# Moving the first block's weight splits to VectorE and interleaving gather and gate/up in the first expert quad

## The chip, the cores and the metric

One core of one Trainium2 chip runs the kernel. The metric is device time in microseconds (us), the median of the runs. The engines are TensorE (PE in the rows; PEld is its weight load), VectorE (DVE), ScalarE (ACT), GpSimd (POOL) and SyncE (SP), whose queue issues nearly all weight transfers.

## What is computed

Two model blocks on 256 rows of 1024 columns, in fp32. The reference, cut to what matters:

```python
def first_block(x, ...):
    h = rms_norm(x, attn_norm_w)
    x = x + hybrid_mixer(h, ...)      # w_in -> conv + state-space branch, causal attention branch, gates, w_out
    h = rms_norm(x, moe_norm_w)
    x = x + hier_moe(h, ...)          # 4 groups x 8 experts, best group, best 2 experts in it
    gate = sigmoid(rms_norm(x, ple_norm_w) @ w_ple_gate)
    ...
def hier_moe(h, ...):
    hid = silu(h @ w_gate[e]) * (h @ w_up[e])
    out += comb[:, e] * (hid @ w_down[e])
def second_block(x, ...):             # long convolution branch, attention branch, gates, w_out
```

## The kernel before

Matrices are multiplied as three products of split numbers: each weight part of 128x1024 is loaded raw (512 KB), a high half `wsh` is made by a rounding copy on ScalarE (`act`, line 152) and a low half `wsl` as raw minus high half, and a product is high x high, high x low and low x high. `Split` (line 209) does this for a chunk of 256 output columns in two parts. Where the low half is made is `pool_lo`: for the parts that the table `APL` (line 46) lists, `G.tensor_tensor` on GpSimd (line 230), otherwise `to_split` on VectorE (`tt`, line 155). `next_a` (line 471) gives `Split` the entry of `APL` for chunk n; `v_chunk` (line 458) asks for entries of its own, and there are none. `APL` lists 19 parts of the chunks 0 to 33. The very first chunk has a fixed split of its own (line 224: part 0 on VectorE, part 1 on GpSimd). The second block lists none.

The first block goes through the convolution inputs (five chunks `pxbc` with their convolution steps `cv`, `th`, `xf` on VectorE and ScalarE, and the chunks of `pv` between them), transposes `xf` (line 569), then takes for each of four head groups the chunks `pq`, `pk`, `pz`, the rotary step (lines 716 to 725, its additions on GpSimd, line 724), a state-space group and an attention group (softmax in `mx`, `pt`, `sm`; transposes line 699), then gates and output projections (`pg`, `pao`, `pso`, `pwo`).

The order on each engine is not the order of the source: a planner lays the instructions out by costs and due times, and `hp(tag)` shifts a due time by the entry of `HPD` (line 47), among them some chunks' loads and splits (`w5` by 300, `w8` and `w16` by 150). Each engine and each queue works its list in order. Matmuls marked by `pmm` (line 867) keep their order of the source on TensorE.

The experts are taken in eight quads of four. A quad (line 1051) makes a one-hot table of its 128 slots (`make_oh`), gathers the rows of x into `xe` by matmuls, two of the eight column groups of 128 at a time (`gather`, line 983, psum tile `pxe`, one half copied by ScalarE, the other by VectorE), multiplies by gate and up weights (`gate_up`, line 1013: 16 matmuls for a pair of column groups, four experts side by side), then makes the hidden layer (`thm`, `hT`), multiplies by the down weights (`pyd`) and scatters (`acc`). `combine_weights` (line 947) works out the slot weights and the overflow count `cnti`, which the weight queue loads into a register (line 1216).

A quad has 24 weight tiles of 512 KB (`eload`, line 375; the load is line 382). They go into pools whose sequence is written out (lines 365 to 373): 9 + 3 x 6 + 4 + 6 + 4 + 6 + 2 = 49 buffers, filled while the first block runs; the 50th load takes the first buffer again. The gate/up tile i of a quad holds two column groups of expert i % 4, so that the first four tiles are free when the column groups 0 and 1 have been used. The first quad's order is:

```python
    if q == 0:
        make_oh(0); gather(0); combine_weights()
    wg, wd = quad_weights(q)
    if not last:
        quad_weights(q + 1); make_oh(q + 1)
    gate_up(q, (0, 1), pg, wg)
    if q == 0: slot_weights(0)
    slot_rows(q)
    for k in range(2, KD, 2): gate_up(q, (k, k + 1), pg, wg)
```

Of the kernel before, what the change touches and what calls it, by code (L numbers as in the profile page):

```python
# [23 lines left out]
KD = 8  # L24
# [18 lines left out]
VH = (0,)  # L43
XS = 256
W0 = 50
APL = {0: (0,), 10: (0,), 16: (0,), 18: (0,), 2: (0,), 22: (1,), 23: (1,), 24: (1,), 26: (1,), 27: (0,), 28: (0,), 31: (0,), 33: (0,), 4: (1,), 5: (0, 1), 6: (0,), 8: (0, 1)}
HPD = {'L1': 300, 'an0': 20, 'ao2': 80, 'ao3': 40, 'as2': -150, 'cgt3': -20, 'chy5': -20, 'clow1': -20, 'cpg1': -300, 'cv1': 20, 'cv4': 300, 'cwo3': 10, 'cza1': 40, 'czh1': -20, 'dt': 80, 'ex2': -10, 'ga00': -80, 'ga02': -10, 'hy3': -20, 'hy4': 40, 'lc0': 80, 'lc1': 20, 'mx2': -40, 'pT1': 300, 'pe3': 300, 'r34': 150, 'rr0': -10, 'rr1': 300, 'siza1': 80, 'sm2': -20, 'so0': -80, 'sq0': -20, 'uo001': -150, 'uo011': -80, 'v2': 10, 've0': -150, 've2': -150, 've3': -10, 'w0': 20, 'w1': -10, 'w11': -150, 'w13': 40, 'w16': 150, 'w17': 300, 'w18': 80, 'w21': 40, 'w24': 150, 'w29': 80, 'w31': -10, 'w5': 300, 'w8': 150, 'w9': -150, 'xc1': -150, 'xc2': -150, 'xc3': -80, 'xo1': 300, 'xo3': -150, 'ye1': -80, 'yn0': 150, 'z1': 10}
WQ = {(1, 0, 0): 10}
PHI = ""
# [78 lines left out]
def tile_two_blocks(ctx: ExitStack, tc: tile.TileContext, a: dict, tap=None, upto="all"):  # L128
# [16 lines left out]
    def hp(tag):  # L145
        return tc.high_priority(HPD[tag]) if tag in HPD else nullcontext()
# [7 lines left out]
    def tt(out, in0, in1, op):  # L154
        return V.tensor_tensor(out=out, in0=in0, in1=in1, op=op)  # L155
# [13 lines left out]
    def psum(tag, shape, name):  # L169
        tag = PTG.get(name, tag)  # L170
        return ps.tile(shape, F32, tag=tag, bufs={"mm": 2, "sc": 4, "tr": 2}[tag], name=name)
# [223 lines left out]
    with ExitStack() as pa:  # L395
# [62 lines left out]
        def v_chunk(j):  # L458
            with hp(f"v{j}"):
                w = w0 if j == 0 else Split(hl, lambda i: a["w_vdt"][2 * j + i], KD, 260, pool_lo=APL.get(f"v{j}", ()))  # L460
            pv = [psum("mm", [P, 260], "pv") for _ in range(NT)]
# [9 lines left out]
        def next_a():  # L471
            n = next(ia)
            with hp(f"w{n}"):
                return Split(hl, lambda i: a["w_a"][2 * n + i], KD, T, pool_lo=APL.get(n, ()))

# [290 lines left out]
        for i in range(4):  # L766
            q = got["q"]
            p = proj(h, "pk")
            with hp(f"k{i}"):
                k = rope(p, "k")  # L770
# [84 lines left out]
    with ExitStack() as pm:  # L855
# [24 lines left out]
        def st(name, *sh, dt=F32):  # L880
            return mo.tile([P, NT, *sh], dt, name=name)
# [65 lines left out]
        def combine_weights():  # L947
            gd, gw, ex, w1, w2 = st("gd", 4), st("gw", 1), st("ex", 1), st("w1", 1), st("w2", 1)
            tt(gd, lg[:, :, 0:4], bc(gm, 4), OP.subtract)
            act(gd, gd, AF.Exp)  # L950
            V.tensor_reduce(out=gw, in_=gd, axis=AX.X, op=OP.add)
            V.reciprocal(gw, gw)
            oh12, tv, vv = st("oh12", 2, 8), st("tv", 2, 8), st("vv", 2, 1)
            for i in range(2):
                ts(oh12[:, :, i, :], rk, float(i), OP.is_equal)
                tt(tv[:, :, i, :], oh12[:, :, i, :], es, OP.mult)
            V.tensor_reduce(out=vv, in_=tv, axis=AX.X, op=OP.add)
            tt(ex, vv[:, :, 1, :], vv[:, :, 0, :], OP.subtract)
            act(ex, ex, AF.Exp)
            ts(w1, ex, 1.0, OP.add)  # L960
            V.reciprocal(w1, w1)
            tt(w1, w1, gw, OP.mult)
            tt(w2, w1, ex, OP.mult)
            ew = st("ew", 1, 8)
            tt(oh12[:, :, 0, :], oh12[:, :, 0, :], bc(w1, 8), OP.mult)
            tt(oh12[:, :, 1, :], oh12[:, :, 1, :], bc(w2, 8), OP.mult)
            tt(ew[:, :, 0, :], oh12[:, :, 0, :], oh12[:, :, 1, :], OP.add)
            for t in R:
                tt(comb4[:, t].rearrange("p (g e) b -> p g e b", g=4), bc(goh[:, t], 8).rearrange("p g (e b) -> p g e b", b=4),
                   ew[:, t].broadcast_to([P, 4, 8]).rearrange("p g (e b) -> p g e b", b=4), OP.mult)  # L970
                V.tensor_copy(comb[:, t, :, 4:5], rstd[:, t : t + 1].rearrange("p (q o) -> p q o", q=1).broadcast_to([P, NQ, 1]))
            V.tensor_reduce(out=cnt, in_=prk[:, 2, :], axis=AX.X, op=OP.max)
            V.tensor_copy(cnti, cnt)
# [5 lines left out]
        def fill():  # L979
            if filler is not None:  # L980
                next(filler, None)

        def gather(q):
            for k in range(0, KD, 2):
                p = psum("tr", [P, 2, P], "pxe")
                for i in range(2):
                    for t in range(NT):
                        pmm(p[:, i, :], x_t[:, t, (k + i) * P : (k + i + 1) * P], ohs[q][:, t, :], t == 0, t == 1)
                act(xe[:, k, :], p[:, 0, :], AF.Copy, scale=vc("moe_norm_w", k))
                ts(xe[:, k + 1, :], p[:, 1, :], vc("moe_norm_w", k + 1), OP.mult)  # L990

        scales, waiting, slots = {}, [], {}

        def slot_weights(q):
            pcs = psum("tr", [P, 5], "pcs")
            for t in range(NT):
                pmm(pcs, ohs[q][:, t, :], comb[:, t, q, :], t == 0, t == 1)
            cj = mo.tile([P, 4], F32, tag="cj", bufs=2, name="cj")
            cs = mo.tile([P, 1], F32, tag="cs", bufs=2, name="cs")
            hr = mo.tile([P, 1], F32, tag="hr", bufs=2, name="hr")  # L1000
            ts(hr, pcs[:, 4:5], 0.5, OP.mult)
            V.tensor_tensor_reduce(cj, pcs[:, 0:4], blk4, 2.0, 0.0, OP.mult, OP.add, cs)
            stt(cs, cs, hr, hr, OP.mult, OP.mult)
            scales[q] = hr, cs

        def slot_rows(q):
            pqt = psum("tr", [P, T], "pqt")
            for t in range(NT):
                ptranspose(pqt[:, t * P : (t + 1) * P], ohs[q][:, t, :])
            slots[q] = Q = mo.tile([P, T], F32 if q == NQ - 1 else F32R, tag="Q", name="Q")  # L1010
            V.tensor_copy(Q, pqt)

        def gate_up(q, ks, pg, wg):
            for k in ks:
                for j in range(4):
                    pmm(pg[32 * j : 32 * j + 32, :], xe[:, k, 32 * j : 32 * j + 32],
                        wg[4 * (k // 2) + j][:, k % 2, :], k == 0, k == KD - 1)
# [33 lines left out]
        def quad(q):  # L1051
            last = q == NQ - 1
            if q == 0:
                make_oh(0)
                gather(0)
                combine_weights()
            wg, wd = quad_weights(q)
            if not last:
                quad_weights(q + 1)
                make_oh(q + 1)  # L1060
            pg = psum("mm", [P, 512], "pgu")
            gate_up(q, (0, 1), pg, wg)
            while waiting:
                waiting.pop()()
            if q == 0:
                slot_weights(0)
            slot_rows(q)
            fill()
            for k in range(2, KD, 2):
                gate_up(q, (k, k + 1), pg, wg)  # L1070
                fill()
            hr, cs = scales.pop(q)
            th = mo.tile([P, T], F32, tag="Yh", name="thm")
            act(th, pg[:, 0:T], AF.Tanh, scale=hr)
            stt(th, th, 1.0, pg[:, 0:T], OP.add, OP.mult)
            stt(th, th, cs, pg[:, T:], OP.mult, OP.mult)
            if last:
                fill()
            else:
                gather(q + 1)  # L1080
            pht = psum("tr", [P, 2, P], "pht")
            for f in range(2):
                ptranspose(pht[:, f, :], th[:, f * P : (f + 1) * P])
            hT = mo.tile([P, 2, P], F32, tag="hT", name="hT")
            act(hT, pht, AF.Copy)
            if not last:
                slot_weights(q + 1)
            py = [psum("mm", [P, 512], f"pyd{c}") for c in range(2)]
            if last:
                down(q, wd, hT, py, (0, 1), (0, 1))  # L1090
                fill()
                last_scatter(q, py)
                return
            down(q, wd, hT, py, (0, 1), (0,))
            add = scatter(q, 0, py[0])
            down(q, wd, hT, py, (0, 1), (1,))
            add()
            waiting.append(scatter(q, 1, py[1]))
            if q == NQ - 2:
                waiting.pop()()  # L1100
# [86 lines left out]
        with ExitStack() as pp:  # L1187
# [29 lines left out]
            with tc.If(nover > CAP), ExitStack() as po_:  # L1217
                ov = pool(po_, "ov")
                ho = tuple(ov.tile([P, KD // 2, T], F32, tag="ho", bufs=2, name="ho") for _ in range(2))
                for k in range(KD):  # L1220
                    xo = mo.tile([P, NT, P], F32, tag="hT", name="xo")
                    ks = slice(k * P, (k + 1) * P)
# [656 lines left out]
```

## Time and profile before

| | us |
|---|---|
| median of 3 runs | 805.27 (805.26 to 809.57) |
| profiled execution | 805.95 |
| its span, first to last instruction | 804.2 |
| TensorE busy | 766.6 (95%) |
| VectorE busy | 478.6 (60%) |
| ScalarE busy | 345.0 (43%) |
| GpSimd busy | 135.1 (17%) |

All times in rows are microseconds from the span's start unless marked ns. A busy TensorE is not TensorE at its peak, since matmuls overlap and their ends are modelled. The granted clock (PEclk) is a share of full speed. A row of a timeline gives start, length, engine, line, operation, out<-in, shape and count, and in brackets the idle time of the engine before it and what ended it. A row of waits gives who waited for whom, the sum in us, the number of times and the longest.

### The profile page before, as it was taken

Reading aid. Unit: us, or ns where it says so; the run is one execution under the profiler, and the core shown is the slowest. Engines: PE = TensorE matmul, PEld = TensorE weight load, DVE = VectorE, ACT = ScalarE, POOL = GpSimd, SP = SyncE. Lnnn points to the kernel's source line nnn. Section 1 sums busy time; section 2 is a strip of 40 time slices with the busy share of each in tenths; the row PEclk is TensorE's granted clock in tenths of the full one; section 3 lists DMA queues with packets and bytes.
Section 4 is the critical chain, followed back from the end, with each engine's and each line's share of the span. In section 5 each row is a group of like instructions: output and inputs, shape, how many; then the busy total and the mean of one; then the engine's idle time right before and its main releaser. Section 6 shows DMA issues by size and latency. Waiting matters only on the chain. (4 is left out here: it accounts for less than half of the span.)

```text
span 804.2 us, 14032 instructions
## 1 busy us (share of the span) xinstructions
PE 766.6 (95%) x5515; PEld 608.9 (76%) x5515; DVE 478.6 (60%) x932; ACT 345.0 (43%) x659; POOL 135.1 (17%) x147
## 2 busy tenths in 40 slices
PE   8996989998999999999999999889999999999997
PEld 7996878786799999645534343249999878888997
DVE  6788767887752555522243433047877887866662
ACT  6573453646544443012113112047757426555541
POOL 3713631333033310000000000100112540000000
PEclk9998999999999999999999999999999999999999
DMA  7653554243279989599999999976445231632561
GB/s 258 219 185 101 184 182 156 84 153 131 80 249 329 346 327 394 227 410 413 382 384 419 417 417 409 393 317 218 124 138 195 95 131 53 191 98 82 175 189 53
DMA packets 53204, 187.19 MB, mean 233 GB/s; under 512 B 5886, under 2 KB 8190, under 8 KB 53071
## 3 DMA queue, kind: packets, MB, share of 16 engines
q1 hardware_dynamic: 52736, 184.93, 63.3%
q0 software_dynamic: 400, 1.34, 0.4%
q8 instruction: 44, 0.72, 0.3%
q14 instruction: 24, 0.20, 0.1%
HBM read 185.20 MB, written 1.05 MB: 232 GB/s over the span
## 5 line engine op out<-in xcount | busy, mean ns | idle before, releaser
L152 ACT ACTIVATE wsh<-w 128x1024 fp32r<-128x1024 f32 (+2 forms) x148 | 153.8, 1043 | 144.4 <-issue 23.4
L155 DVE TENSOR_TENSOR wsl<-w,wsh 128x1024 fp32r<-128x1024 f32 (+3 forms) x127 | 155.8, 1231 | 67.8 <-ACT wsh L152 67.5
L143 PE MATMUL pgu<-we,xe 128*32 128x512 f32 x512 | 79.9, 599 | 4.3 <-DMA we<-in_w_e 4.0
L143 PEld LDWEIGHTS pgu<-we,xe 128*32 128x32 f32 x512 | 17.6, 109 | 55.2 <-issue 30.4
L230 POOL TENSOR_TENSOR wsl<-w,wsh 128x1024 fp32r<-128x1024 f32 x19 | 45.9, 2418 | 71.6 <-ACT wsh L152 71.4
L143 PE MATMUL pg<-h,wsh 128*128 128x256 f32 x256 | 47.1, 284 | 0.0
L143 PEld LDWEIGHTS pg<-h,wsh 128*128 128x128 f32 x256 | 39.6, 189 | 0.4 <-issue 0.2
L143 PE MATMUL pwo<-wsh,mh 128*128 128x256 f32 x128 | 36.1, 283 | 0.5 <-DVE x_t L164 0.5
L143 PE MATMUL pg<-h,wsl 128*128 128x256 f32 x128 | 36.2, 283 | 0.0
L143 PEld LDWEIGHTS pxe<-oh,x_t 128*128 128x128 f32 x256 | 30.0, 191 | 8.1 <-issue 4.2
L143 PE MATMUL pwo<-wsl,mh 128*128 128x256 f32 x128 | 36.1, 283 | 0.0
L143 PE MATMUL pwo<-wsh,ml 128*128 128x256 f32 x128 | 35.9, 282 | 0.0
L143 PE MATMUL pxe<-oh,x_t 128*128 128x128 f32 x256 | 33.0, 283 | 0.9 <-DVE xe L159 0.9
L143 PE MATMUL pyd<-we,hT 128*32 128x512 f32 x256 | 31.7, 597 | 1.2 <-ACT hT L152 0.7
L164 DVE SCALAR_TENSOR_TENSOR thm<-thm,pgu 128x256 f32<-128x256 f32 x8 | 3.4, 422 | 48.1 <-ACT thm L152 48.1
L143 PE MATMUL pq<-h,wsh 128*128 128x256 f32 x128 | 29.1, 319 | 0.0
L143 PE MATMUL pxbc<-h,wsh 128*128 128x256 f32 x160 | 28.5, 281 | 0.0
L1191 POOL DMA_DIRECT2D pT__5280<-in_p x1 | 0.8, 792 | 150.7 <-DMA we<-in_w_e 150.7
L155 DVE TENSOR_TENSOR Yl<-pyd,Yh 128x512 fp32r<-128x512 f32 x14 | 9.7, 692 | 27.4 <-ACT Yh L152 27.4
L143 PE MATMUL pz<-h,wsh 128*128 128x256 f32 x128 | 25.6, 291 | 0.0
L143 PEld LDWEIGHTS pq<-h,wsh 128*128 128x128 f32 x128 | 21.3, 204 | 5.5 <-issue 4.0
L143 PEld LDWEIGHTS pwo<-wsh,mh 128*128 128x128 f32 x128 | 24.3, 190 | 0.7 <-DVE x_t L164 0.7
(473 smaller groups left out, 2125.0 us busy)
## 6 DMA issues: line engine op xcount, KB each, us to landing
we<-in_w_e SPq DMA_DIRECT2D x192, 512.0 KB, 10.0
w<-in_w_a SPq DMA_DIRECT2D x74, 512.0 KB, 4.2
w<-in_w_c SPq DMA_DIRECT2D x66, 512.0 KB, 3.8
w<-in_w_vdt SPq DMA_DIRECT2D x8, 520.0 KB, 4.0
x_t<-in_x SPq DMA_DIRECT2D x2, 512.0 KB, 4.6
raw_ple<-in_w_ple POOLq DMA_DIRECT2D x2, 512.0 KB, 8.7
w<-in_w_c SPq DMA_DIRECT2D x2, 384.0 KB, 3.2
out<-x_t SPq DMA_DIRECT2D x3, 256.0 KB, 2.4
```

Of the source, the lines that this page charges most:

```text
L143: return PE.matmul(out=out, lhsT=lhsT, rhs=rhs, start=start, stop=stop, **k)
L152: return S.activation(out=out, in_=in_, func=func, **k)
L155: return V.tensor_tensor(out=out, in0=in0, in1=in1, op=op)
L164: return V.scalar_tensor_tensor(out=out, in0=in0, scalar=s, in1=in1, op0=op0, op1=op1)
L230: G.tensor_tensor(out=lo, in0=raw, in1=hi.bitcast(F32), op=OP.subtract)
L1191: G.dma_start(pT, a["p"])
```

## The change

The table `APL` is emptied, so all splits of `next_a` are made on VectorE. `gather` takes the column pairs as an argument. In the first quad alone, gather and gate/up alternate by column pairs, and `combine_weights`, `slot_weights` and `slot_rows` come after the third gate/up. The other quads run as before.

```diff
-APL = {0: (0,), 10: (0,), 16: (0,), 18: (0,), 2: (0,), 22: (1,), 23: (1,), 24: (1,), 26: (1,), 27: (0,), 28: (0,), 31: (0,), 33: (0,), 4: (1,), 5: (0, 1), 6: (0,), 8: (0, 1)}
+APL = {}
...
-        def gather(q):
-            for k in range(0, KD, 2):
+        def gather(q, ks=range(0, KD, 2)):
+            for k in ks:
...
             if q == 0:
                 make_oh(0)
-                gather(0)
-                combine_weights()
             wg, wd = quad_weights(q)
             if not last:
                 quad_weights(q + 1)
                 make_oh(q + 1)
             pg = psum("mm", [P, 512], "pgu")
-            gate_up(q, (0, 1), pg, wg)
-            while waiting:
-                waiting.pop()()
             if q == 0:
+                gather(0, (0, 2))
+                gate_up(0, (0, 1), pg, wg)
+                gather(0, (4,))
+                gate_up(0, (2, 3), pg, wg)
+                gather(0, (6,))
+                gate_up(0, (4, 5), pg, wg)
+                combine_weights()
                 slot_weights(0)
-            slot_rows(q)
-            fill()
-            for k in range(2, KD, 2):
-                gate_up(q, (k, k + 1), pg, wg)
+                slot_rows(0)
+                gate_up(0, (6, 7), pg, wg)
+            else:
+                gate_up(q, (0, 1), pg, wg)
+                while waiting:
+                    waiting.pop()()
+                slot_rows(q)
                 fill()
+                for k in range(2, KD, 2):
+                    gate_up(q, (k, k + 1), pg, wg)
+                    fill()
```

## Rows read from the trace of the kernel before

**Rows 1.** Busy time by stage: window, length, engines, clock, DMA share, GB/s.
```profile
0.00:320.00 320.00, 303.38 (x2358) 279.02 (x2358) 215.46 (x387) 159.62 (x300) 99.67 (x87) 0.99 0.60 211
338.00:536.00 198.00, 187.20 (x1170) 80.27 (x1163) 60.20 (x153) 38.76 (x79) 4.09 (x16) 1.00 1.02 404
```
**Rows 2.** The chain that ended last, shares in 495 to 545 us.
```profile
by line: DMA we<-in_w_e 56.4%; PE acc L143 9.6%; PE pyd L143 9.3%; PE ptr L340 4.8%; PE ppg L143 2.2%; ACT wsh L152 2.1%; ACT junk L152 2.1%; ACT gh L152 1.7%; issue 1.4%; DVE x_t L155 0.9%; ACTq L152 0.2%; SPq L382 0.1%
```
**Rows 3.** Busy time by stage, the hole in the stream.
```profile
329.00:338.00 9.00, 8.37 (x74) 6.03 (x78) 5.54 (x38) 1.67 (x5) 0.00 (x0) 1.00 0.08 30
```
**Rows 4.** SyncE's queue: its wait in 330 to 341 us; issues, 331 to 339.
```profile
SPq L382 <- PE pgu L143: 6.4, 3, 5.0
...
L382 SPq DMA_DIRECT2D we<-in_w_e x4: 332/382/383, 336.8 to 338.2; - x4
```
**Rows 5.** Timeline of TensorE, first quad.
```profile
330.99 3.95 PE L143 MATMUL pxe<-oh,x_t 128*128 128x128 f32 x32
334.88 1.92 PE L143 MATMUL pgu<-we,xe 128*32 128x512 f32 x16
```
**Rows 6.** Timeline of VectorE, first quad.
```profile
330.90 0.15 DVE L973 CAST cnti<-cnt 128x1 int32<-128x1 f32 x1
...
332.49 0.35 DVE L159 TENSOR_SCALAR xe<-pxe,vec 128x128 f32<-128x128 f32 x1 [0.17 <-ACT xe L152]
```
**Rows 7.** Groups of GpSimd, 0 to 320 us: busy us, mean ns, idle before.
```profile
L230 POOL TENSOR_TENSOR wsl<-w,wsh 128x1024 fp32r<-128x1024 f32 x19 | 45.9, 2418 | 71.6 <-ACT wsh L152 71.4
L724 POOL TENSOR_TENSOR kr<-rA,rB 32x256 f32<-32x256 f32 x16 | 15.8, 988 | 19.6 <-DVE kr L155 18.8
```
**Rows 8.** Groups of VectorE, 0 to 320 us.
```profile
L155 DVE TENSOR_TENSOR wsl<-w,wsh 128x1024 fp32r<-128x1024 f32 (+1 forms) x61 | 76.4, 1256 | 45.3 <-ACT wsh L152 45.1
```
**Rows 9.** Timeline of GpSimd, 55 to 72 us.
```profile
55.89 2.44 POOL L230 TENSOR_TENSOR wsl<-w,wsh 128x1024 fp32r<-128x1024 f32 x1 [17.62 <-ACT wsh L152]
59.67 4.73 POOL L230 TENSOR_TENSOR wsl<-w,wsh 128x1024 fp32r<-128x1024 f32 x2 [1.34 <-ACT wsh L152]
69.22 2.37 POOL L230 TENSOR_TENSOR wsl<-w,wsh 128x1024 fp32r<-128x1024 f32 x1 [4.81 <-ACT wsh L152]
```
**Rows 10.** Timeline of VectorE, 44 to 84 us.
```profile
48.40 1.52 DVE L164 SCALAR_TENSOR_TENSOR cv<-u,cw,cv 128x256 f32<-128x256 f32 x3
...
55.99 2.38 DVE L164 SCALAR_TENSOR_TENSOR e<-dtr 128x32 f32<-128x32 f32 x1
58.30 0.17 DVE L159 TENSOR_SCALAR dt<-dtr 128x32 f32<-128x32 f32 x1
...
59.73 2.38 DVE L159 TENSOR_SCALAR pl<-sq 128x32 f32<-128x32 f32 x1
62.14 3.67 DVE L164 SCALAR_TENSOR_TENSOR pl<-pl,sq 128x32 f32<-128x32 f32 x7
...
68.22 3.65 DVE L164 SCALAR_TENSOR_TENSOR cv<-u,cw,cv 128x256 f32<-128x256 f32 x3
```
**Rows 11.** Who waited for whom, TensorE, 0 to 320 us.
```profile
PE pxt L569 <- DVE xf L164: 6.2, 2, 4.3
```
**Rows 12.** Busy time in three stretches of the first block; third number from the end: clock.
```profile
68.00:72.00 4.00, 3.26 (x15) 3.06 (x15) 3.86 (x5) 1.72 (x4) 2.37 (x1) 0.61 0.00 0
74.00:78.00 4.00, 4.00 (x24) 4.00 (x23) 2.01 (x5) 1.20 (x2) 0.00 (x0) 0.57 0.14 56
...
100.00:120.00 20.00, 17.77 (x124) 14.48 (x123) 13.71 (x35) 10.02 (x31) 7.03 (x7) 1.00 0.51 185
```
**Rows 13.** Timelines around two softmax waits, VectorE and TensorE.
```profile
106.40 2.23 DVE L159 TENSOR_SCALAR mx<-mx 128x8 f32<-128x8 f32 x1
...
112.98 0.30 PE L699 MATMUL ptp<-cst,pt 128*128 128x128 f32 x1 [2.23 <-DVE pt L159]
...
186.20 2.12 DVE L159 TENSOR_SCALAR pt<-pt,sm 128x256 f32<-128x256 f32 x1
...
188.37 0.44 PE L699 MATMUL ptp<-cst,pt 128*128 128x128 f32 x2 [1.18 <-DVE pt L159]
```

## The prediction

> **What bounds the kernel now.** I read four views in this order: the busy times by stage, the chain that ended last, the DMA share around the idle spot it points to, and then who waits for whom. By stage [rows 1], TensorE is busy 303.38 of the first 320 us: the first block is bound by TensorE, and only its gaps can be won. From 338 to 536 us the DMA share is 1.02 at 404 GB/s: the expert stage is bound by the transfer of its weights. The chain agrees: over 495 to 545 us, 56.4% of it is expert weights arriving [rows 2]. So a microsecond counts in the expert stage only if it lets the stream of weights begin earlier, and the stream has one hole: from 329 to 338 us its share is 0.08 [rows 3]. All 49 buffers that exist before the first quad are full, and the next load waits for a release. The queue that issues loads spends 5.0 us at a stretch waiting for a gate/up matmul, and the first four loads go out at 336.8 to 338.2 us [rows 4]. After 338 us the stream hardly pauses, so what moves 336.8 moves the end, and a gain in the first block, which comes before the hole, passes through in full: the hole is 9 us long and the stream is idle in it anyway.
>
> **Part two, the interleave.** Before, the first quad gathers all eight columns (32 matmuls from 330.99), and the first 16 gate/up matmuls start at 334.88 [rows 5]: (334.88 - 330.99) / 32 = 0.122 us each. With 16 gathers ahead of them instead of 32 they start at 330.99 + 16 x 0.122 = 332.94, and are done 1.94 us earlier. The first load issues at 336.81 - 1.94 = 334.87. The later releases come soon enough: 16 + 16 + 8 + 8 matmuls in the new order put the second batch's end some 1.6 us earlier, and four loads at one per about 1.3 us (512 KB at 404 GB/s) keep the stream busy for 5 us in between. The total of TensorE work in the quad is unchanged, so the hidden layer is ready at the same time, and it does not bound. Term: **-1.9 us**.
>
> What it could cost: the first gate/up matmuls now follow closely on the copies of their columns. In before, the second column is copied at 332.49 for 0.35 us [rows 6], so it is ready at 332.84, 0.1 us ahead of the 332.94 at which the first (and 0.5 us later its own) matmul wants it. The combine weights are now traced behind 48 of the gate/up matmuls, but VectorE is idle for most of 334 to 343 us and fits them in; the slot weights that need them come at about 340.5. One wait does move: the register load on the weight queue waits for the overflow count, which VectorE writes at 330.90 [rows 6], and the 50th load is queued behind it. Unless the count slips beyond 334.8, nothing is lost; bounds 0 to +1.9, I take 0 because 0.15 us of work has 4 us of room.
>
> **Part one, the splits.** Nineteen of the first block's low-half splits go from GpSimd (2.418 us each) to VectorE [rows 7]. On VectorE the same operation takes 1.256 us, the mean of 61 (1.23 undisturbed) [rows 8]. That adds 19 x 1.23 = 23.4 us to an engine busy 215.46 of 320 us [rows 1], so at first sight it is the wrong way. What speaks for it is how VectorE runs while a GpSimd split is under way. GpSimd splits run at 55.89, twice from 59.67 and at 69.22 [rows 9]. In just these moments a tensor_scalar of 128x32 takes 2.38 us where its like takes 0.17 a moment before, seven small ones take 3.67 us in place of about 1.3, and three convolution taps take 3.65 where three took 1.52 at 48.40 [rows 10]. VectorE stands still until GpSimd is done. Each split thus costs VectorE about 2.2 us here (with the one at 55.99, four times: 8.7 us), against 1.23 if VectorE did it itself (4.9 us): **3.8 us net**. And this is where TensorE waits: 6.2 us for the convolution's output in two waits, the longer 4.3 [rows 11]. Three of the four splits lie ahead of the first wait, one ahead of the second, so all 3.8 us come off: about 1.4 us of the first wait and 1.1 of the second are left. Bounds: 0 (the splits land ahead of the same chain with a wait of their own) and -6.2 (both waits vanish).
>
> The clock goes with it. In 68 to 72 us the granted clock averages 0.61 and in 74 to 78 it is 0.57 [rows 12]: parts at 1.2 GHz after those waits. Lost: 3.26 x 0.39 = 1.3 us and 4 x 0.43 = 1.7 us. I count the first fall as gone, its wait being cut to a third, and the second as kept, its wait being cut by half only: **-1.3 us**, bounds 0 and -3.0.
>
> Two more locks lie ahead of softmax waits. At 106.40 the scaling of the maxima takes 2.23 us in place of 0.15, and TensorE then waits 2.23 us at 112.98; at 186.20 a probability scaling takes 2.12 in place of 0.35, and TensorE waits 1.18 at 188.37 [rows 13]. With the split in VectorE's queue each is worth 2.08 - 1.23 = 0.85 and 1.77 - 1.23 = 0.54: **-1.4 us**, bounds 0 and -3.3 (the split queued behind the chain).
>
> The other 13 splits I cost at nothing. Nine run between 232 and 294 us, where TensorE has no wait of note and VectorE is about half idle; four (14, 36, 89 to 97, 171 us) lie beside full TensorE work. Without that cover a split costs 1.23 each. Against the sum stands the order: the planner that lays out all engines by cost and due time now sees other costs, and the due times of some of these chunks place their splits in front of the chain. I put one split with its wait on the path: **+1.2 us**, bounds 0 and what the last rival says.
>
> *A rule against it.* GpSimd's rotary additions average 0.988 us in the key group [rows 7]; nothing in TensorE's main waits is theirs. The Trainium skill (SBUF — State Buffer, Who interferes with whom) says that a VectorE instruction with two SBUF inputs contends with a GpSimd instruction that reads SBUF, the second one blocking whole. By it the moved splits would hold up the additions in turn, an estimate of up to 1.2 us for each of the five splits between 80 and 190 us; the sum would then be -1.2 instead of -7.2 if every one lay on the path. The long mean of the additions agrees with the rule, the missing wait says that it costs nothing here.
>
> **Sum.** -1.9 - 3.8 - 1.3 - 1.4 + 1.2 = -7.2 us. The profiled execution took 805.95 us (span 804.2), 0.7 above the median of 805.27, so 798.75 by its own time and 798.1 against the median.
>
> **The rivals.**
> *More than the sum: waits and clock go together.* If both falls of the clock vanish, 1.7 us more are won, and without an extra split on the path 1.2 more: -10.1, 795.2. For it: one wait of 2.23 us, at 112.98, was followed by no fall (100 to 120 us has a granted clock of 1.00 [rows 12]), and the waits left at 68 and 73 would be shorter. Against: the second fall came after only about 2 us of waiting. The Trainium skill (TensorE: Matmul & The Clock Gate, Part 1) says that activity releases the throttle and its lack restores it; the trace agrees, with 0.61 after the longest wait. By that rule shorter waits alone would bring both back.
>
> *Only the interleave counts.* The splits queue on VectorE where the locks were, each with a wait for ScalarE's half, and the first block ends when it did: -1.9, 803.4. For it: VectorE already idles 45.3 us in front of its 61 splits [rows 8], 0.74 us each, so one really occupies 1.97 us, close to the 2.2 of a lock.
>
> *Slower: VectorE's queue is blocked at its head.* GpSimd sat idle 71.4 us in front of its 19 splits waiting for ScalarE [rows 7], 3.8 us each, at no cost to anyone. VectorE works in order: with a split at the head that waits for ScalarE, the convolution and softmax steps behind it wait too, and TensorE for them. Place: the nine splits from 55 to 190 us. On the path the locks return 8.7 + 2.1 + 1.8 = 12.6 us and the interleave 1.9, 14.5 together; nine splits at 1.6 us each take that back, and from there on it is slower. At 1.97 us each it is +17.7 - 14.5 = +3.2: 808.5. At 2.5 us each it passes 1%. Against: due times put most splits well ahead of use, and at 3.8 us the wait was GpSimd's because it had nothing else to do. The Trainium skill (Perfetto Trace Analysis, Optimizing Scalar/DVE Operations) says that offloading may make sense where VectorE is saturated, but that GpSimd shares a port with it and it might not help; at 67% busy it is not saturated here.
>
> *The interleave does nothing.* The register load on the weight queue waits for a count that now comes after the gate/up matmuls, and the stream starts when it did: -7.2 + 1.9 = -5.3, 800.0.
>
> **How the numbers follow.** Forecast (798.1, itself 795 to 801.5) 0.40; more than the sum 0.25; only the interleave 0.17; slower 0.13; no interleave 0.05. About 1% (8.05 us) is what a measurement of this kernel can tell from no change. Faster by more, below 797.2: the whole of the first rival and a third of the forecast, 0.25 + 0.13 = 0.38. Slower by more, above 813.3: the part of the slower case beyond 2.5 us per split, 0.05. Within 1%: 0.57. The range runs from 792 (the first rival with most of the softmax waits gone as well) to 808.5 (the slower case at 1.97 us); about 0.13 lies outside.
>
> **What would show it.** Right: no GpSimd split but the one in the first chunk; VectorE's small steps near 60 us at 0.2 us each; TensorE's waits for the convolution's output down from 6.2 to about 2.4 us; the first block done some 5 us earlier; expert loads resuming about 1.9 us sooner after the router's last matmul than now; and the stream gapless after that. Wrong: the same or larger waits of TensorE for VectorE in the first block with splits just ahead of them, a hole in the stream still 9 us long, or TensorE waiting in the quad for the copies of its columns.

## The result, and the profile after

The changed kernel takes 796.1 us (median of 4 runs), the kernel before 805.26 beside it: ratio 0.987 (95% interval 0.984 to 0.990), so 1.3% faster; that is past the 1% bound, to which the forecast gave 0.38. Timed once more in a later session it was 795.14 against 806.11, ratio 0.985 (0.982 to 0.988). The forecast was 798.1 with a range of 792 to 808.5. The profiled execution took 796.15 us, its span 794.0, which is 10.2 less than before. The forecast's direction and places were right; three of its five terms were too small, and the loss that it allowed for was there, but for another reason.

Busy times by stage, after, answering to [rows 1] and [rows 12] (columns as there):

```profile
0.00:320.00 320.00, 308.65 (x2427) 283.76 (x2428) 221.16 (x437) 160.31 (x301) 53.30 (x69) 0.99 0.64 220
...
68.00:72.00 4.00, 4.00 (x37) 3.97 (x36) 4.00 (x8) 2.40 (x4) 0.00 (x0) 1.00 0.08 13
74.00:78.00 4.00, 4.00 (x35) 3.72 (x34) 3.90 (x9) 1.95 (x4) 2.35 (x3) 1.00 0.94 348
...
204.00:207.00 3.00, 2.24 (x8) 1.74 (x9) 2.71 (x10) 2.14 (x5) 0.00 (x0) 0.56 0.24 97
...
338.00:536.00 198.00, 184.21 (x1145) 83.72 (x1144) 66.48 (x162) 46.29 (x92) 4.81 (x17) 0.99 1.00 396
```

In these 320 us GpSimd lost 46.4 us of busy time (99.67 to 53.30) and VectorE gained only 5.7 (215.46 to 221.16), though it took over 19 splits of 1.23 us, 23.4 us together. The stage also holds other work now (50 more instructions of VectorE, of which 19 are splits), since all comes earlier. The page of the whole execution is free of that:

```profile
PE 760.6 (96%) x5515; PEld 606.4 (76%) x5515; DVE 478.7 (60%) x951; ACT 345.6 (44%) x659; POOL 88.0 (11%) x128
```

VectorE is busy 478.7 us with 951 instructions, and it was 478.6 with 932. So nearly all of the 23.4 us had been busy time before in which VectorE stood still. Both clock falls of [rows 12] are gone (0.61 and 0.57, now 1.00), and a new one stands at 204 us (0.56). The expert stage is bound as before, with a DMA share of 1.00.

TensorE's waits in the first 330 us (sum in us, times, longest), where [rows 11] had 6.2 us for `xf`:

```profile
PE pao L143 <- ACT tg L152: 4.6, 1, 4.6
PE ptp L699 <- DVE pt L159: 1.4, 3, 0.9
...
PE pxt L569 <- DVE xf L164: 0.5, 1, 0.5
```

VectorE's timeline, 56 to 70 us, where [rows 10] had four long stalls:

```profile
56.34 1.22 DVE L155 TENSOR_TENSOR wsl<-w,wsh 128x1024 fp32r<-128x1024 f32 x1
...
58.52 0.18 DVE L159 TENSOR_SCALAR pl<-sq 128x32 f32<-128x32 f32 x1
...
59.07 1.23 DVE L155 TENSOR_TENSOR wsl<-w,wsh 128x1024 fp32r<-128x1024 f32 x1
...
62.08 1.23 DVE L155 TENSOR_TENSOR wsl<-w,wsh 128x1024 fp32r<-128x1024 f32 x1
...
63.32 0.42 DVE L164 SCALAR_TENSOR_TENSOR xf<-th,cv 128x256 f32<-128x256 f32 x1
...
66.27 0.41 DVE L164 SCALAR_TENSOR_TENSOR xf<-th,cv 128x256 f32<-128x256 f32 x1
...
69.21 1.22 DVE L155 TENSOR_TENSOR wsl<-w,wsh 128x1024 fp32r<-128x1024 f32 x1
```

The step on `sq` takes 0.18 us where it took 2.38. Three splits stand ahead of the first `xf`; the fourth comes behind both and holds up nobody.

Groups on VectorE and on GpSimd in the first 320 us, answering to [rows 8] and [rows 7]:

```profile
L155 DVE TENSOR_TENSOR wsl<-w,wsh 128x1024 fp32r<-128x1024 f32 (+1 forms) x80 | 101.0, 1264 | 40.7 <-ACT wsh L152 40.5
```

```profile
L724 POOL TENSOR_TENSOR kr<-rA,rB 32x256 f32<-32x256 f32 x16 | 15.8, 990 | 20.8 <-DVE kr L155 19.9
```

With 80 splits in place of 61 VectorE idles 40.7 us in front of them, less than the 45.3 before: the 19 more did not add to the time in which a split at the head of its queue waits for ScalarE's half.

Around the first softmax wait, VectorE and TensorE, answering to [rows 13]:

```profile
97.68 0.16 DVE L159 TENSOR_SCALAR mx<-mx 128x8 f32<-128x8 f32 x1
97.75 1.22 DVE L155 TENSOR_TENSOR wsl<-w,wsh 128x1024 fp32r<-128x1024 f32 x1
```

```profile
102.29 0.30 PE L699 MATMUL ptp<-cst,pt 128*128 128x128 f32 x1 [0.25 <-DVE pt L159]
```

The new wait at 200 us, on TensorE and on ScalarE:

```profile
204.76 0.58 PE L143 MATMUL pao<-ath,wsh 128*128 128x256 f32 x1 [4.63 <-ACT tg L152]
```

```profile
200.61 0.40 ACT L152 ACTIVATE pt<-pt,mx 128x128 f32<-128x128 f32 x1 [3.59 <-DVE mx L159]
...
204.04 0.19 ACT L152 ACTIVATION_READ_ACCUMULATOR pt<-pt,mx 128x1 f32 x1
204.13 0.57 ACT L152 ACTIVATE tg<-pg 128x512 f32<-128x512 f32 x1
```

The tanh `tg`, whose `pg` was complete at about 200.1, stands in ScalarE's list behind eight exponentials, which themselves waited for VectorE until 200.61. TensorE needs the psum that it frees.

The first quad on TensorE, SyncE's waits and the hole, answering to [rows 5], [rows 4] and [rows 3]:

```profile
323.09 1.95 PE L143 MATMUL pxe<-oh,x_t 128*128 128x128 f32 x16
324.97 1.92 PE L143 MATMUL pgu<-we,xe 128*32 128x512 f32 x16
```

```profile
L382 SPq DMA_DIRECT2D we<-in_w_e x5: 328/382/538, 326.9 to 329.8; - x5
```

```profile
SPq L1224 <- DVE w L159: 6.5, 1, 6.5
SPq L382 <- PE pgu L143: 4.1, 3, 2.6
```

```profile
322.00:324.00 2.00, 2.00 (x23) 1.90 (x22) 1.72 (x13) 0.20 (x1) 0.00 (x0) 1.00 0.05 18
324.00:327.00 3.00, 3.00 (x27) 1.44 (x26) 1.68 (x10) 0.73 (x2) 0.00 (x0) 1.00 0.01 3
```

The loads behind the hole start at 326.9 us, when the first 16 gate/up matmuls are done. Between the 49th load and the 50th lie 9.8 us (317.1 to 326.9), and 11.8 before (325.0 to 336.8): the hole is 2.0 us shorter.

Where the time went, by comparing first starts (before, after): `pac`, a matmul behind the transposes of `xf` and the chunk `pq`, 80.09 to 71.37 (8.7 us won); behind the first softmax wait the lead is 10.2 to 10.3 (`pg` 181.24 to 170.97, 10.27); at the end of the first block 7.9; the first gate/up matmul 334.88 to 324.97 (9.9); the first load behind the hole 336.81 to 326.90 (9.9); the end 10.2. What is won ahead of the hole reaches the end in full.

### The profile page after: what moved, and what is told of

The parts are those of the page before. It is cut to its first block, busy times and chain, and to the rows that moved or that the text cites. A ratio compares the mean times of both kernels' runs of the same rounds, so it can differ in the third digit from the quotient of the medians.

```text
span 794.0 us, 14043 instructions
## 1 busy us (share of the span) xinstructions
PE 760.6 (96%) x5515; PEld 606.4 (76%) x5515; DVE 478.7 (60%) x951; ACT 345.6 (44%) x659; POOL 88.0 (11%) x128
## 5 line engine op out<-in xcount | busy, mean ns | idle before, releaser
L155 DVE TENSOR_TENSOR wsl<-w,wsh 128x1024 fp32r<-128x1024 f32 (+3 forms) x146 | 180.4, 1239 | 63.3 <-ACT wsh L152 62.9
L143 PE MATMUL pgu<-we,xe 128*32 128x512 f32 x512 | 76.1, 598 | 4.2 <-DMA we<-in_w_e 4.1
L143 PE MATMUL pq<-h,wsh 128*128 128x256 f32 x128 | 26.8, 302 | 0.0
L143 PE MATMUL pv<-wsh,h 128*128 128x260 f32 x128 | 24.3, 286 | 0.5 <-ACT h L152 0.5
L143 PEld LDWEIGHTS pg<-h,wsl 128*128 128x128 f32 x128 | 24.2, 189 | 0.5 <-issue 0.5
L143 PEld LDWEIGHTS pxbc<-h,wsh 128*128 128x128 f32 x160 | 24.5, 189 | 0.0
```

The lines of the kernel that those rows point to most:

```text
L143: return PE.matmul(out=out, lhsT=lhsT, rhs=rhs, start=start, stop=stop, **k)
```

## The experiments

All were timed in five rounds beside the kernel before (806.06 in the first session, 806.11 in the second, 806.05 in the third). Expectations stand as they were written before each run. The first edit is against the kernel before, all others are against the changed kernel.

**Splits alone.** The new table with the old first quad.

```diff
-APL = {0: (0,), 10: (0,), 16: (0,), 18: (0,), 2: (0,), 22: (1,), 23: (1,), 24: (1,), 26: (1,), 27: (0,), 28: (0,), 31: (0,), 33: (0,), 4: (1,), 5: (0, 1), 6: (0,), 8: (0, 1)}
+APL = {}
```

> The table of GpSimd splits is emptied, the first quad keeps its old order. Lock theory (a GpSimd split holds VectorE up, and TensorE behind it): the first block ends about 8 us sooner, as in the changed kernel, the first gate/up matmul comes 8 us sooner, and the time is 805.3 - 8 = about 797.5. Rival (only the interleave counts): 805, within 1 us of the kernel before.

It took 798.74 us, ratio 0.990 (0.988 to 0.993). `pac` comes 8.89 us earlier than in the kernel before, `pg` 10.4, the first gate/up 7.2 and the end 7.85; the wait for `tg` is there with 4.74 us. The splits carry 7 to 8 of the 10 us, and the new wait came with them.

**Interleave alone.** The table `APL` of before and the new first quad (`gather` with its argument, the alternation for q == 0):

```diff
-APL = {}
+APL = {0: (0,), 10: (0,), 16: (0,), 18: (0,), 2: (0,), 22: (1,), 23: (1,), 24: (1,), 26: (1,), 27: (0,), 28: (0,), 31: (0,), 33: (0,), 4: (1,), 5: (0, 1), 6: (0,), 8: (0, 1)}
```

> The first quad is interleaved, the 19 GpSimd splits stay. Both theories of part one expect the first block unchanged, the first gate/up matmul 1.9 to 2.0 us sooner, the stream of expert weights resuming 1.9 us sooner and the time 2 us shorter, 803.3. If the stream were not the bound of the expert stage: 805.3.

It took 804.21 us, ratio 0.998 (0.996 to 1.000): its time alone does not tell it from nothing. TensorE's timeline does; first the row of the kernel before, then this run:

```profile
329.63 0.43 PE L143 MATMUL prk<-asg,bits 128*128 128x32 bf16 x5 [1.15 <-DVE asg L155]
```

```profile
335.06 0.42 PE L143 MATMUL prk<-asg,bits 128*128 128x32 bf16 x5 [1.15 <-DVE asg L155]
...
338.30 1.92 PE L143 MATMUL pgu<-we,xe 128*32 128x512 f32 x16
```

From the router's last matmuls to the first gate/up it takes 3.24 us; before, 329.63 to 334.88, 5.25. The interleave is worth 2.0 us; this execution had come 5.4 us late to the router, with more falls of the clock ahead of it.

**The four splits of 55 to 72 us back on GpSimd.** The order of ScalarE's work and of the weight queue's is the changed kernel's, and TensorE's differs in a few rows.

```diff
-APL = {}
+APL = {4: (1,), 5: (0, 1), 6: (0,)}
```

> The changed kernel with four of the 19 splits back on GpSimd (chunks 4, 5 twice, 6: those at 55 to 72 us). Lock theory: VectorE's small steps there last 2.4 us again, TensorE waits 5 to 6 us for the convolution's output, the clock falls again, the first block ends 8 to 9 us later than in the changed kernel: 804 to 805. Order theory (the gain came from a new order of all 19): most of the gain stays, 797 to 799.

It took 803.07 us, ratio 0.996 (0.994 to 0.998), a little under the range of the lock theory and far from the other. TensorE's timeline and two stretches of the stages:

```profile
68.23 1.97 PE L569 MATMUL pxt<-cst,xf 128*128 128x128 f32 x8 [4.25 <-DVE xf L164]
...
73.47 0.44 PE L569 MATMUL pxt<-cst,xf 128*128 128x128 f32 x2 [1.77 <-DVE xf L164]
```

```profile
68.00:72.00 4.00, 3.46 (x15) 3.17 (x15) 3.86 (x5) 1.73 (x4) 2.36 (x1) 0.57 0.00 0
74.00:78.00 4.00, 4.00 (x37) 4.00 (x36) 2.94 (x5) 1.86 (x3) 0.00 (x0) 1.00 0.14 56
```

The four splits bring the waits for `xf` back to 6.0 us (0.5 without them) and the first clock fall too: `pac` is 7.2 us later than in the changed kernel, and 1.52 earlier than in the kernel before in place of 8.72. The 1.5 that stay are about the second fall (1.7 by the prediction's working), which did not come here after the wait of 1.77.

**Is it the port, or the work?** Two kernels leave the splits on VectorE and give GpSimd work in the same four places whose result nobody uses: one subtraction that reads two tiles, or two memsets that only write.

```diff
...
+                for i in {4: (1,), 5: (0, 1), 6: (0,)}.get(n, ()):
+                    G.tensor_copy(dm[:, 0:1], w.parts[i][0][:, 0, 0:1].bitcast(F32))
+                    G.tensor_tensor(out=dm, in0=x_t[:, 0, :], in1=x_t[:, 1, :], op=OP.subtract)
...
```

The tile `dm` takes the result. The one-column copy ties the place to the high half of the split. The other kernel has, in place of the last line:

```diff
+                    for _ in range(2):
+                        G.memset(dm, 0.0)
```

> The changed kernel with four GpSimd subtractions of 128x1024 added at 55 to 72 us, of the splits' own length, that read two SBUF operands and whose result nobody uses; each begins when the high half of one of the four splits is there. Lock theory: VectorE's small steps beside them take 2.4 us again, TensorE waits for the convolution's output again, now with the four splits in VectorE's queue as well: 7 to 10 us more than the changed kernel. Order theory: nobody waits for them, within 1 us of the changed kernel.

> As the run with the added subtractions, but each is replaced by two memsets of 128x1024, which only write. If GpSimd stops VectorE only where both read: within 1 us of the changed kernel. If any GpSimd work of this length does it: as with the subtractions, scaled by its length.

With subtractions it took 804.67 us, 9.5 more than the changed kernel in the same session; with memsets 796.98, 1.8 more, which lies between its two expectations and near the first. GpSimd, VectorE and TensorE with subtractions:

```profile
56.45 3.46 POOL L478 TENSOR_TENSOR dm<-x_t 128x1024 f32<-128x1024 f32 x1
...
60.23 2.40 POOL L478 TENSOR_TENSOR dm<-x_t 128x1024 f32<-128x1024 f32 x1
```

```profile
57.55 2.39 DVE L159 TENSOR_SCALAR den<-e 128x32 f32<-128x32 f32 x1
...
60.36 2.32 DVE L155 TENSOR_TENSOR sv<-e,den 128x32 f32<-128x32 f32 x1
```

```profile
70.27 1.97 PE L574 MATMUL pxt<-cst,xf 128*128 128x128 f32 x8 [6.08 <-DVE xf L164]
```

GpSimd and VectorE with memsets:

```profile
59.17 1.97 POOL L479 MEMSET dm<- 128x1024 f32 x2
...
61.96 1.96 POOL L479 MEMSET dm<- 128x1024 f32 x2
```

```profile
59.19 0.97 DVE L159 TENSOR_SCALAR pl<-sq 128x32 f32<-128x32 f32 x1
...
61.78 0.48 DVE L164 SCALAR_TENSOR_TENSOR cv<-u,cw,cv 128x256 f32<-128x256 f32 x1
62.17 0.18 DVE L164 SCALAR_TENSOR_TENSOR pl<-pl,sq 128x32 f32<-128x32 f32 x1
```

A VectorE step of either kind that starts while the GpSimd subtraction runs lasts until that has ended: 2.39 and 2.32 us for steps of 0.17 and 0.19. Beside a memset, which only writes, a `tensor_scalar` is held (0.97 for 0.18), and the steps with two inputs pass at 0.48 and 0.18. So the waits for `xf` come from GpSimd's reading beside VectorE's steps, and not from a new order: TensorE's order in both runs is the changed kernel's. The Trainium skill (SBUF — State Buffer, Who interferes with whom) says of steps with two inputs just this: a VectorE operation with two SBUF inputs contends with GpSimd operations that read, and not with ones that only write. The numbers of both runs agree.

**The tanh ahead of the exponentials.** The changed kernel with a higher priority for `tg`.

```diff
-            act(tg, p, AF.Tanh, scale=0.5)
+            with tc.high_priority(300):
+                act(tg, p, AF.Tanh, scale=0.5)
```

> The changed kernel with the due time of the gate's tanh (tile tg) brought forward by 300. Queue theory of the new wait (the tanh stands on ScalarE behind eight exponentials of the softmax, and TensorE waits 4.6 us at 200 us for its psum buffer): the wait goes, the half clock after it too, 4 to 6 us less than the changed kernel. Rival (TensorE there waits for the softmax in any case, the tanh only ends later): the wait turns up a few us later at the transposes ptp, and the time stays within 1 us of the changed kernel.

It took 795.03 us, ratio 0.986 (0.983 to 0.988): no gain on the changed kernel in the same session (795.14, below). Neither expectation came as written. The wait fell from 4.63 to 2.00 (the tanh still stands behind two of the exponentials), it did not turn up at `ptp` (1.4 us as before), and the first gate/up came 3.06 us sooner. In the last quad the first gate/up is still 3.2 us sooner (492.08, 495.27 in the changed kernel), but the last down matmul ends only 0.6 sooner and the span is only 0.7 shorter. Waits of SyncE's queue in 495 to 520 us, its timeline, and a wait of TensorE in 500 to 530 us:

```profile
SPq L1226 <- SPq L1226: 6.8, 3, 5.2
```

```profile
500.21 4.07 SPq L382 DMA_DIRECT2D we<-in_w_e  x4
512.41 0.81 SPq L248 DMA_DIRECT2D w<-in_w_c  x2
513.33 0.84 SPq L382 DMA_DIRECT2D we<-in_w_e  x2
```

```profile
PE pyd L143 <- DMA we<-in_w_e: 2.5, 1, 2.5
```

The planner had moved the overflow branch (line 1226) ahead of the last two expert loads. The queue stands there for 6.8 us, and its two long waits end as loads issued before it land (510.1 and 511.4 us). The DMA share of 510 to 515 us falls to 0.67, the last two loads go out from 513.33 instead of 510.18, and TensorE waits 2.5 us for them. The gain was won, and given back at that branch.

**The changed kernel again**, in that session.

> The changed kernel itself, for comparison beside the others: ratio 0.987 to the kernel before, as in its first runs.

It took 795.14 us, ratio 0.985, with the same waits and 4.74 us for `tg`; both clock falls at 68 to 78 us are gone here too (1.00). The new wait belongs to the kernel, not to one execution.

**Ten late splits back on GpSimd**, those of the chunks 16 to 33.

```diff
-APL = {}
+APL = {16: (0,), 18: (0,), 22: (1,), 23: (1,), 24: (1,), 26: (1,), 27: (0,), 28: (0,), 31: (0,), 33: (0,)}
```

> The changed kernel with the ten late splits (chunks 16 to 33, from 171 us on) back on GpSimd, the nine early ones on VectorE. Lock theory: the 8.7 us won by 72 us and 1.5 at the softmax wait near 105 us stay; the softmax waits near 185 us come back (about 3 us), and the new wait of 4.6 us at 200 us, which stands behind them, may go: 794 to 797. If the late splits matter by themselves: they cost what GpSimd's longer time costs, over 798.

It took 793.27 us, ratio 0.984 (0.981 to 0.987), a little under the first range. The softmax waits of 171 to 178 us are back (1.3 and 1.2), the wait for `tg` is gone, and a lead of 10.24 us on the kernel before lasts to the end of the first block. Either those splits cost something on VectorE, or they changed the planner's order. The next runs tell that apart.

**Only the chunks 16 and 18 on GpSimd; all ten but 18; all ten again.** With 16 and 18 alone, TensorE, ScalarE and the weight queue have the very order of the kernel with ten, and the eight splits after 220 us move to VectorE. The second has the table of ten without the entry of 18, the third is the kernel with ten once more.

```diff
-APL = {}
+APL = {16: (0,), 18: (0,)}
```

> The changed kernel with only the chunks 16 and 18 (their splits ran at 160.99 and 175.58 us in the run of the ten late splits) left on GpSimd; the eight splits after 220 us are on VectorE. TensorE, ScalarE and the weight queue then have the very order of the kernel with ten late splits, and only VectorE and GpSimd differ, after 220 us. Theory A (the new wait at 200 us came from the order that the planner chose, not from the work on VectorE; the splits after 220 us cost nothing on either engine): no wait for the tanh at 200 us, first gate/up matmul 2.3 us before that of the changed kernel, 792.5 to 794.5 us, the same as the run with ten late splits. Theory B (the eight later splits on VectorE are what costs the changed kernel its 2.4 us): first gate/up matmul as in the changed kernel, 795 to 796.5 us.

> The changed kernel with the ten late splits on GpSimd but that of chunk 18, which ran at 175.58 us beside a probability scaling of 2.11 us; the planner orders TensorE, ScalarE and the weight queue anew. Lock theory alone: the softmax waits of 4.1 us at 171 to 178 us become shorter by 0.9 to 2 us and the kernel takes 791 to 792.5 us. Order theory: what the new order does decides; with a wait for a tanh behind the exponentials again, the 2 us are given back and it takes 794 to 796 us.

> The kernel with the ten late splits on GpSimd once more, to put the two runs above beside it on the same chip: 792.5 to 794.5 us, ratio 0.983 to 0.986.

The kernel with two took 792.52 us, ratio 0.984 (0.981 to 0.987); with ten again 794.28, 0.986 (0.984 to 0.988); with nine 797.87, 0.991 (0.988 to 0.993), above both ranges of its expectation. With two, TensorE's waits to 330 us, the stretch where the clock had fallen, and the first quad:

```profile
PE ptp L699 <- DVE pt L159: 4.6, 8, 1.3
```

```profile
204.00:208.00 4.00, 4.00 (x23) 2.51 (x23) 2.96 (x7) 2.04 (x4) 0.00 (x0) 1.00 0.17 31
```

```profile
322.40 1.92 PE L143 MATMUL pgu<-we,xe 128*32 128x512 f32 x16
```

The eight splits cost nothing on either engine (first gate/up at 322.40; with ten in that session 322.63), as the forecast had it for splits beside idle VectorE. The order did it: with the two on GpSimd there is no wait for `tg`, and the first gate/up is 2.6 us before the changed kernel's, although 4.6 us of softmax waits stay. With nine the planner made another order. The softmax waits at 173 to 178 us are shorter, 1.5 us in place of 3.2, as the lock theory had it. But a new one of 2.0 us stands at 205.88, the granted clock of 172 to 180 us is 0.79, and the overflow branch is again ahead of two loads. Its waits, SyncE and then TensorE, 480 to 540 us:

```profile
SPq L1225 <- SPq L1225: 6.9, 3, 5.2
...
PE pyd L143 <- DMA we<-in_w_e: 3.4, 2, 3.2
```

By the traces the versions with two and with ten are equal in that session (spans of 790.2 and 790.1 us) and ahead of the changed kernel (794.0 and 793.7). By the times both medians are below the changed kernel's, but the intervals overlap its own (0.982 to 0.988), so that lead is shown by the traces and not by the times.

## Why the prediction was right, and where its sizes were off

- *The bound.* This was right: gains ahead of the hole came through (9.9 us at the first gate/up, 9.9 at the first load behind it, 10.2 at the end).
- *Interleave, -1.9.* This was right: -2.0 in the runs with and without the splits. The copies of the columns held up nothing. The register load waited 6.5 us (6.2 before) and was through at about 324.3, and the 50th load, which stands behind it, went out at 326.9 as soon as gate/up released it.
- *Locks at 55 to 72 us, -3.8.* The mechanism was right, shown by the four splits put back and by the idle subtractions. The size was too small: the waits fell by 5.7 (6.2 to 0.5). The sum charged all four splits at 1.23 to the path of `xf`; the planner put the fourth behind it, at 69.21. The rest of the difference lies in the order of small steps and was not separated.
- *Clock, -1.3.* This was too small: the forecast kept the second fall, and both went, -3.0 by its own working (1.3 and 1.7), and also as 8.7 at `pac` less 5.7 of waits. This is the first rival's half of the story. Its rule, that shorter waits alone bring both back, fits both executions of the changed kernel; no run changed the clock by itself.
- *Softmax locks, -1.4.* This was too small: 1.55 at the first (10.27 less 8.72) against 0.85, because the split ended up behind the scaling (97.75 after 97.68) and not ahead of it. At the second place TensorE waited 3.2 us in all from 183 to 189 us and waits 0.9 now, against 0.54. Over the first block TensorE's softmax waits fell from 6.6 to 1.4 us.
- *Thirteen other splits, 0.* Eight of them, and not nine, run from 232 to 294 us, and five lie earlier (14, 36, 89, 97 and 171 us). That they cost nothing was right for the eight, as the kernel with two shows. It was not right for chunk 16 (171 us): moved together with chunk 18, which the softmax term holds, it changed the order.
- *Give-back, +1.2.* This was right in sign and wrong in what it is: not a split in front of a chain, but ScalarE's list, with `tg` behind eight exponentials, 4.6 us of waiting and a granted clock of 0.56 behind it. Less the softmax waits saved at the second place, it comes to 2.4 net (10.27 to 7.9).
- *The sum.* With the sizes found it is -2.0 - 5.7 - 3.0 - 1.55 + 2.4 = -9.9, as at the first gate/up, against -7.2. That the forecast missed the time by only 2 us is in part luck: gains that were larger than forecast met a loss that was larger too, of a cause that it had not seen.
- *The rule on the rotary additions.* The mean of the key group is 990 ns, 988 before; that of the query group, 916, was 852, which is 1.0 us in all for 16 additions. No wait of TensorE is theirs.
- *Rivals.* "Only the interleave" falls with the run of the splits alone (798.74 us), "blocked at its head" with the idle time of 40.7 us in front of 80 splits; "the interleave does nothing" falls with the 2.0 us in the traces with and without the splits. "More than the sum" was right on the clock and wrong on no give-back; the result, 796.1, lies between it and the forecast.

## What to carry to other kernels

When a small step of VectorE takes as long as the GpSimd instruction beside it, count the GpSimd instruction as VectorE's time. Moving it to VectorE then frees GpSimd and need not lengthen VectorE's busy time (here 478.6 and 478.7 us), and it counts most ahead of a wait of TensorE. Price a move also by the clock falls behind the waits that it removes (here 3.0 us beside 5.7 of waits). Where a planner orders all engines, look after each change for what it moved elsewhere: here a tanh behind exponentials and a branch ahead of two loads cost some 2.5 us each, more than the interleave won.

## What the runs showed of the hardware beyond that

- The hold goes both ways. The idle subtraction that began at 56.45, just behind a VectorE split (56.41, 1.22 us), took 3.46 us, where the one at 60.23 took 2.40: there GpSimd waited for VectorE.
- A GpSimd memset of 128x1024 (0.98 us) held a VectorE `tensor_scalar` of 0.17 us to 0.89 and 0.97, and no step with two SBUF inputs beside it. Work that only writes was thus much cheaper beside the convolution steps (1.8 us for eight memsets) than work that reads (9.5 us for four subtractions).
- A branch on a loaded value in the queue of weight loads held it for 6.8 and 6.9 us in two kernels while loads ahead of it landed, and TensorE then waited 2.5 and 3.2 us for the last loads. In the changed kernel, where the branch comes some 20 us earlier, the same wait is 7.2 us in six pieces, the longest 1.3, and TensorE has no such wait for the last loads.
- After similar waits the clock did not always fall: 1.77 us at 73.47 was followed by a granted clock of 1.00 in 74 to 78 us, where the kernel before had 0.57 in that stretch after a wait of 1.98.
